# Stick-breaking attention with filler projections: the order of transpositions, first scores, filler and meta weights in a hybrid decoder layer

## The chip, the cores and the metric

The kernel runs on one core of a Trainium2 chip. The metric is device time in microseconds (us) of one execution. Engines are named as the profile names them: PE (TensorE, matrix products and transpositions), PEld (its weight loads), DVE (VectorE), ACT (ScalarE), POOL (GpSimd), SP (SyncE, which issues the DMA transfers).

## What is computed

One layer of a hybrid decoder: a sequence of 512 tokens with 16 learned meta tokens put in front (528 rows), width 1024, all in float32. The input is normalised and projected by `w_in`. From the projections, a gated chunkwise retention with 4 heads and a stick-breaking attention with 16 heads of width 64 are made; each passes an output projection and is multiplied by a sigmoid gate of its own, the sum goes through `w_out`, and a SwiGLU FFN follows. The change touches only the part in which the attention is computed, and the gate projections that are computed beside it:

```
def stick_breaking(q, k, v):
    ...
    for i in range(Lp // CHUNK):
        ...
        z = jnp.einsum('bhtd,bhsd->bhts', q_blk, k_pre) * scale
        ...
        log_not = jnp.where(valid, jax.nn.log_sigmoid(-z), 0.0)
        after = lax.cumsum(log_not, axis=3, reverse=True) - log_not
        a = jnp.where(valid, jnp.exp(jax.nn.log_sigmoid(z) + after), 0.0)
        outs.append(jnp.einsum('bhts,bhse->bhte', a, v_pre))
```

Each block of 128 queries attends to all keys before it, the 16 meta tokens among them. A weight is the sigmoid of its own score times the product of the sigmoids of the negated scores of all keys between it and the query.

## The kernel before

**Numbers in two halves.** TensorE multiplies in a short format here, so each float32 operand is split into a high half (ACT copies it, L104) and a low half (DVE subtracts, L101), and one product becomes three matmuls: high by high, low by high, high by low. One such group of three, for 128 of the depth, is called a triple here. A weight arrives by a DMA into `raw`, and its halves are `wh` and `wl`. In the scores, `ka` and `qa` are high halves of keys and queries and `kl` is the low half of the keys; only two matmuls are needed per score, since a tile of 128 rows holds both halves of a head of 64.

**A head.** The sixteen heads are taken as eight pairs; (p, h) below is half h of pair p. For a head there are four scores, one for each query block, from the longest (block 3, 528 keys, in two matmul pairs, since a bank holds 512 numbers) to the shortest (block 0, 144 keys). `score` (L600) does one: the matmuls on PE into banks `px`, sigmoids of the score and of its negative on ACT (L623, L624), a scan on DVE that makes the running products (L626), and a product on DVE that makes the weights `sp` (L627). `turn` (L644) transposes the weights on PE into a bank `pb` (L98), which ACT and DVE split into `ah` and `al`. `turn_meta` (L630) does the weights of the 16 meta keys apart: POOL copies and subtracts them into the tile `mg`, DVE transposes it into `x` (L639), POOL copies the result into `am`. `values` (L654) multiplies with the values on PE, and ACT and DVE add the two halves into `ysb` (L663, L664). Banks: `px` has three, of which the longest score takes two and each of the others and each value product one; `pb` has two.

**The order of the work.** PE would stand while DVE and ACT work on a score, so `head` (L692) writes out one head's transpositions and value product and the next head's scores as one list of pieces, each with a weight, and `run` (L807) places filler between the pieces in proportion to the weights: triples of projections, which need nothing of attention. z is a score, t a transposition, tm the meta weights, pv the value product; the number is the block:

```
            q, g = (p, 1) if hd == 0 else (p + 1, 0)
            seq = (
                (1.0, z, 3), (1.3, t, 3), (1.3, t, 2), (1.3, z, 2), (0.2, t, 1), (0.8, z, 1), (1.2, tm, 0), (1.8, t, 0),
                (1.4, z, 0), (1.2, pv, 0),
            )
```

So in the list of a first half (p, 0) the scores are those of (p, 1), and in that of a second half (p, 1) they are those of the next pair, (p + 1, 0). The filler comes from a queue of work (`Work`, L351), one item after the other. It holds, for each pair, the projections named in `FILL` (L778) for that pair, and then q and k of the pair after next (`qk_work`, L503). The items "b1", "b2" are gate projections of one block of 128 features (`gate_work`, L547: 8 triples, a sigmoid L555 and a store L556), "b45" and the like are gates of two blocks at once (`gates_work`, L560), and "v" is half of the values of two pairs. An item's weight is loaded when the item ahead of it begins. Before the loop over pairs (L817) an opening run (L816) computes the four scores of head (0, 0) with 8 triples of filler, of which 3/7 stand ahead of the first score. In pair 7 there is no next pair: both heads' pieces are one list, with what remains of the filler, and "a2" is left over for the time behind it. In pairs 1 to 5, `tm` also issues token sums on POOL, which a later stage needs.

From here to the end of attention PE's instructions stand in the order in which the code issues them. On DVE, ACT, POOL and SP a scheduler orders them. Behind attention, the sums `ysb` are split into `yh` and `yl`, and the projection by `w_sb_out` follows.

## Time and profile before

| what | value |
|---|---|
| median of 3 runs | 1211.29 us (1210.54 to 1212.5) |
| the profiled execution's own time | 1211.73 us |
| its span, from the first instruction to the last | 1209.9 us |
| mean granted clock of TensorE | 0.991 of full speed |
| scan L626, 64 of them | 59.8 us of DVE, 936 ns each on average |
| splits of weights `wl<-raw,wh` L101, 202 of them | 267.9 us of DVE, 1335 ns each on average |
| traffic of the DMA | 118.26 MB, mean 98 GB/s |

An engine's share says how much of the span it was busy; a DMA-issuing, waiting or branching instruction isn't counted as busy. In the lists of a timeline a line has the start of an instruction, its length, the engine, the line of code, the operation, what it writes and reads, and in brackets how long the engine had stood before it and which instruction ended that. The granted clock is the share of full speed at which TensorE was allowed to run: at half of it a matmul takes twice as long.

### The profile page before, as it was taken

The numbers are of one execution on the slowest core, as the hardware profiler recorded it, in microseconds if no ns is written. First come the engines' busy times: TensorE is split into PE (matmuls) and PEld (weight loads), VectorE is DVE, ScalarE is ACT, GpSimd is POOL, SyncE is SP. The second block draws the span as 40 slices with busy tenths as digits, with TensorE's granted clock in tenths as the row PEclk, the third lists the DMA queues.
The fourth block names the chain that finished last, engine by engine and source line by source line (L and its number), as shares of the span: only waits on it lengthen the run. The fifth ranks groups of instructions, "written<-read, shape, count | busy, mean of one in ns | idle before, by whom it ended". The sixth has DMA issues, their size and how long they took to land.

```text
span 1209.9 us, 18875 instructions
## 1 busy us (share of the span) xinstructions
PE 1174.2 (97%) x7629; PEld 1067.0 (88%) x7629; DVE 869.3 (72%) x1138; ACT 537.1 (44%) x905; POOL 387.2 (32%) x386
## 2 busy tenths in 40 slices
PE   7989999999999999999999999999999999999997
PEld 7877898889789998998899899778999999998886
DVE  6588898987536785586678657776899999983333
ACT  5477676755424434343333424334454444443221
POOL 2036668552032330340323020000265666620000
PEclk9989999999999999999999999999999999999999
DMA  6321211214643214132321425324222333353211
GB/s 194 86 72 53 70 48 41 70 45 139 213 138 130 70 46 138 36 95 89 105 71 45 139 70 154 133 87 157 71 80 95 106 105 106 108 178 114 94 46 70
DMA packets 94504, 118.26 MB, mean 98 GB/s; under 512 B 2488, under 2 KB 71104, under 8 KB 94416
## 3 DMA queue, kind: packets, MB, share of 16 engines
q1 hardware_dynamic: 93984, 115.98, 29.5%
q8 instruction: 60, 0.98, 0.3%
q10 hardware_dynamic: 432, 1.07, 0.3%
q14 instruction: 28, 0.23, 0.1%
HBM read 109.96 MB, written 7.08 MB: 97 GB/s over the span
## 4 chain that ended last, share of the span: by engine, by line
PE 77%; DVE 9%; POOL 3%; ACT 3%; issue 2%; DMA 1%; DVEq 0%; POOLq 0%; ACTq 0%; SPq 0%
PE pp L95 33%; PE pb L95 19%; PE pa L95 18%; PE pc L95 4%; DVE wl L101 3%; PE pb L98 2%; DVE sm L626 2%; PE px L95 2%; ACT wh L104 1%; DVE sp L627 1%; DMA raw<-in_w_in_dram 1%; POOL raw L260 1%; DVE kl L101 1%; POOL st L260 1%; DMA raw<-in_w_sb_out_dram 1%
## 5 line engine op out<-in xcount | busy, mean ns | idle before, releaser
L101 DVE TENSOR_TENSOR wl<-raw,wh 128x1024 fp32r<-128x1024 f32 (+1 forms) x202 | 267.9, 1335 | 78.7 <-ACT wh L104 75.2
L104 ACT ACTIVATE wh<-raw 128x1024 fp32r<-128x1024 f32 (+1 forms) x202 | 201.7, 1008 | 252.9 <-PE pp L95 85.7
L95 PE MATMUL pp<-hT,wh 128*128 128x512 f32 (+2 forms) x308 | 109.1, 354 | 1.4 <-DVE qb L101 1.2
L95 PE MATMUL pp<-hL,wh 128*128 128x512 f32 (+2 forms) x308 | 105.2, 342 | 0.0
L95 PE MATMUL pp<-hT,wl 128*128 128x512 f32 (+2 forms) x308 | 105.0, 341 | 0.0
L260 POOL TENSOR_TENSOR st<-raw 128x512 f32<-128x512 f32 x28 | 42.5, 1539 | 162.6 <-DMA raw<-in_w_in_dram 162.6
L101 DVE TENSOR_TENSOR wl<-st,wh 128x1024 fp32r<-128x1024 f32 x54 | 84.3, 1565 | 11.8 <-ACT wh L104 11.8
L95 PE MATMUL pp<-qk,wh 128*128 128x512 f32 x256 | 83.1, 399 | 2.0 <-ACT qk L104 1.7
L95 PE MATMUL pp<-wh,hT 128*128 128x256 f32 (+1 forms) x240 | 75.9, 317 | 0.7 <-ACT hT L104 0.7
L95 PE MATMUL pp<-wh,hL 128*128 128x256 f32 (+1 forms) x240 | 74.8, 312 | 0.8 <-DVE ss L147 0.8
L95 PE MATMUL pp<-wl,hT 128*128 128x256 f32 (+1 forms) x240 | 74.4, 310 | 0.0
L104 ACT ACTIVATE wh<-st 128x1024 fp32r<-128x1024 f32 x54 | 55.9, 1055 | 33.6 <-POOL st L260 20.5
L148 POOL TENSOR_TENSOR rs<-rs,nhalf 128x1 f32<-128x1 f32 x20 | 12.4, 618 | 171.0 <-DVE rs L147 171.0
L95 PEld LDWEIGHTS pp<-hT,wh 128*128 128x128 f32 x308 | 59.6, 193 | 7.0 <-issue 1.8
L626 DVE TENSOR_TENSOR_SCAN sm<-sm,mask 128x528 f32<-128x528 f32 (+1 forms) x64 | 59.8, 936 | 8.1 <-ACT sm L623 7.8
L95 PEld LDWEIGHTS pp<-hT,wl 128*128 128x128 f32 x308 | 59.4, 193 | 6.3
L95 PEld LDWEIGHTS pp<-hL,wh 128*128 128x128 f32 x308 | 59.5, 193 | 4.1
L95 PE MATMUL pa<-hL,wh 128*128 128x264 f32 (+1 forms) x192 | 61.6, 321 | 0.0
L95 PE MATMUL pa<-hT,wl 128*128 128x264 f32 (+1 forms) x192 | 61.6, 321 | 0.0
L95 PE MATMUL pa<-hT,wh 128*128 128x264 f32 (+1 forms) x192 | 61.6, 321 | 0.0
L95 PEld LDWEIGHTS pp<-qk,wh 128*128 128x128 f32 x256 | 47.6, 188 | 13.4 <-ACT qk L104 2.4
L101 DVE TENSOR_TENSOR gl<-gt,gh 128x512 fp32r<-128x512 f32 x22 | 16.0, 732 | 50.0 <-ACT gh L104 49.9
(333 smaller groups left out, 3845.8 us busy)
## 6 DMA issues: line engine op xcount, KB each, us to landing
raw<-in_w_in_dram SPq DMA_DIRECT2D x31, 1024.0 KB, 5.1
raw<-in_w_ffn_in_dram SPq DMA_DIRECT2D x22, 1024.0 KB, 5.1
raw<-in_w_in_dram SPq DMA_DIRECT2D x26, 512.0 KB, 4.1
raw<-in_w_ffn_out_dram SPq DMA_DIRECT2D x11, 1024.0 KB, 5.0
raw<-in_w_ret_out_dram SPq DMA_DIRECT2D x8, 1024.0 KB, 5.1
raw<-in_w_sb_out_dram SPq DMA_DIRECT2D x4, 1024.0 KB, 7.2
raw<-in_w_out_dram SPq DMA_DIRECT2D x4, 1024.0 KB, 5.1
ysb<-in_x_dram SPq DMA_DIRECT2D x4, 512.0 KB, 8.6
```

What stands on the lines that cost most here:

```text
L95: return keep(nc.tensor.matmul(*args, **kw))
L98: return keep(nc.tensor.transpose(dst, src, idn))
L101: nc.vector.tensor_tensor(lo, src, hi.bitcast(F32), op=ALU.subtract)
L104: ins = nc.scalar.activation(hi, src, AF.Copy)
L148: nc.gpsimd.tensor_tensor(dst, dst, nhalf[:n], op=ALU.pow)
L260: nc.gpsimd.tensor_tensor(d[:, k : k + 2], p[:, k : k + 2], q[:, k : k + 2], op=op)
L626: nc.vector.tensor_tensor_scan(rev, rev, mask[:, r0:][:, ::-1], 0.0, op0=ALU.mult, op1=ALU.max)
L627: nc.vector.tensor_tensor(sp, sp, sm[:, r0 + 1 : L + 1], op=ALU.mult)
```

## The change

It has three parts. **(1)** The opening run gets two projections' worth of filler instead of one: the gate "b0" goes ahead of q and k of pair 1, twice the columns are placed between the scores of (0, 0), and "b3" moves from the end of pair 7 to pair 0. **(2)** In the list of a second half, the transpositions t3 and t2 stand ahead of the next pair's first score z3 instead of behind it; the weight of each piece goes with it. **(3)** `turn_meta` becomes two functions: `split_meta`, the work of POOL into `mg`, is called behind the last score of a head, and `turn_meta` keeps the transposition on DVE and POOL's copies, at the place of `tm`.

```
-        def turn_meta(hd, att):
+        def split_meta(att):
             g = s2.tile([P, NT, 32], F32R, tag="mg", name="mg", bufs=1)
-            x = s2.tile([P, NT, 32], F32, tag="vs", name="x", bufs=1)
             for i in range(0, NT, 2):
...
                 nc.gpsimd.tensor_copy(g[:, two, 0:NM], m)
                 nc.gpsimd.tensor_tensor(g[:, two, NM:], m, g[:, two, 0:NM].bitcast(F32), op=ALU.subtract)
+            return g
+
+        def turn_meta(hd, g):
+            x = s2.tile([P, NT, 32], F32, tag="vs", name="x", bufs=1)
             nc.vector.transpose(x.rearrange("p a b -> p (a b)"), g.rearrange("p a b -> p (a b)").bitcast(F32))
...
         def z(p, hd, i):
             atts[p][hd][i] = score(p, hd, i)
+            if i == 0:
+                metas[p][hd] = split_meta(atts[p][hd])
...
         def tm(p, hd, j):
-            turn_meta(hd, atts[p][hd])
+            turn_meta(hd, metas[p][hd])
...
-            seq = (
-                (1.0, z, 3), (1.3, t, 3), (1.3, t, 2), (1.3, z, 2), (0.2, t, 1), (0.8, z, 1), (1.2, tm, 0), (1.8, t, 0),
-                (1.4, z, 0), (1.2, pv, 0),
-            )
+            ahead = ((1.0, z, 3), (1.3, t, 3), (1.3, t, 2)) if hd == 0 else ((1.3, t, 3), (1.3, t, 2), (1.0, z, 3))
+            seq = (*ahead, (1.3, z, 2), (0.2, t, 1), (0.8, z, 1), (1.2, tm, 0), (1.8, t, 0), (1.4, z, 0), (1.2, pv, 0))
...
-        FILL = [["b0"], ["b1"], ["v"], ["v"], ["v"], ["v"], ["b2"], ["b45", "b67", "a01", "b3"]]
+        FILL = [["b3"], ["b1"], ["v"], ["v"], ["v"], ["v"], ["b2"], ["b45", "b67", "a01"]]
...
         work = Work()
+        fill(work, 0, ["b0"])
         qk_work(work, 1)
...
-        run([(3.0, lambda: None)] + [(1.0, lambda i=i: z(0, 0, i)) for i in (3, 2, 1, 0)], KD * 3 * T)
+        run([(3.0, lambda: None)] + [(1.0, lambda i=i: z(0, 0, i)) for i in (3, 2, 1, 0)], 2 * KD * 3 * T)
```

What this does to the order of the instructions is shown at three places. A name's number tells one tile from another of the same name; the numbers differ between the two kernels.

The first place is DVE in the opening, from the second score's scan on. `sm` is a score's sigmoid, with the scan's result in it, and `sp` the weights; 528, 400, 272 and 144 columns are blocks 3, 2, 1 and 0. Before:

```order
L627 TENSOR_TENSOR sp_713<-sp_713,sm0_126 128x528
L626 SCALAR_TENSOR_TENSOR sm1_128<-sm1_128,mask_118 128x400
L626 SCALAR_TENSOR_TENSOR sm2_130<-sm2_130,mask_118 128x272
L627 TENSOR_TENSOR sp_713<-sp_713,sm1_128 128x400
L626 SCALAR_TENSOR_TENSOR sm0_126<-sm0_126,mask_118 128x144
L627 TENSOR_TENSOR sp_736<-sp_736,sm2_130 128x272
L627 TENSOR_TENSOR sp_736<-sp_736,sm0_126 128x144
L101 TENSOR_TENSOR wl_1121<-raw_1118,wh_1120 128x1024
L639 STREAM_TRANSPOSE x_859<-mg_858 128x128
```

And after the change:

```order
L627 TENSOR_TENSOR sp_722<-sp_722,sm0_126 128x528
L101 TENSOR_TENSOR wl_1095<-raw_1092,wh_1094 128x1024
L626 SCALAR_TENSOR_TENSOR sm1_128<-sm1_128,mask_118 128x400
L627 TENSOR_TENSOR sp_722<-sp_722,sm1_128 128x400
L626 SCALAR_TENSOR_TENSOR sm2_130<-sm2_130,mask_118 128x272
L627 TENSOR_TENSOR sp_764<-sp_764,sm2_130 128x272
L626 SCALAR_TENSOR_TENSOR sm0_126<-sm0_126,mask_118 128x144
L627 TENSOR_TENSOR sp_764<-sp_764,sm0_126 128x144
L643 STREAM_TRANSPOSE x_897<-mg_782 128x128
L101 TENSOR_TENSOR wl_1160<-raw_1157,wh_1159 128x1024
```

Each scan is now followed by its own product, and two splits of weights, in place of one, stand between the first product and the next thing that DVE does for head (0, 0): one of them behind the first product, the other behind the transposition of the meta weights.

The second place is PE at the start of the list of the second half (6, 1), behind the value product of (6, 0). `px<-ka,qa` and `px<-kl,qa` are the scores of (7, 0), `pb<-ident,sp` transpositions of (6, 1), `pp` filler. Before:

```order
L95 MATMUL px_3045<-ka_2927,qa_2915 128x264
L95 MATMUL px_3045<-kl0_134,qa_2915 128x264
L95 MATMUL px_3048<-ka_2927,qa_2915 128x264
L95 MATMUL px_3048<-kl0_134,qa_2915 128x264
L95 MATMUL pp_3026<-hT_83,wh_2923 128x512
L95 MATMUL pp_3026<-hL_84,wh_2923 128x512
L95 MATMUL pp_3026<-hT_83,wl_2924 128x512
L98 MATMUL pb_3061<-ident_73,sp_2842 128x128
L95 MATMUL pp_3026<-hT_83,wh_2923 128x512
L95 MATMUL pp_3026<-hL_84,wh_2923 128x512
L95 MATMUL pp_3026<-hT_83,wl_2924 128x512
L98 MATMUL pb_3070<-ident_73,sp_2842 128x128 x2
```

And after:

```order
L98 MATMUL pb_3084<-ident_73,sp_2881 128x128
L95 MATMUL pp_3065<-hT_83,wh_2962 128x512
L95 MATMUL pp_3065<-hL_84,wh_2962 128x512
L95 MATMUL pp_3065<-hT_83,wl_2963 128x512
L98 MATMUL pb_3093<-ident_73,sp_2881 128x128 x2
L95 MATMUL pp_3065<-hT_83,wh_2962 128x512
L95 MATMUL pp_3065<-hL_84,wh_2962 128x512
L95 MATMUL pp_3065<-hT_83,wl_2963 128x512
L95 MATMUL px_3103<-ka_2966,qa_2954 128x264
L95 MATMUL px_3103<-kl0_134,qa_2954 128x264
L95 MATMUL px_3106<-ka_2966,qa_2954 128x264
L95 MATMUL px_3106<-kl0_134,qa_2954 128x264
```

The two transpositions, with the triples that belong to them, now stand ahead of z3, whose four matmuls come last here. The next instruction after this piece is the second score of (7, 0), `px_3116<-ka_2966,qa_2954 128x400`, with no triple between; before, the triples and the transpositions lay between the two scores.

The third place is DVE at the end of pair 7. `go` is a gate projection's sum, `al` the low half of a transposition of (7, 1), and the two `wl` splits belong to `w_sb_out`, the weight of the stage behind attention. Before:

```order
L101 TENSOR_TENSOR wl_3649<-raw_3646,wh_3648 128x1024
L101 TENSOR_TENSOR al_3599<-pb_3594,ah_3598 128x384
L573 TENSOR_TENSOR go_3508<-pp_3590,go_3508 128x512
L101 TENSOR_TENSOR wl_3699<-raw_3696,wh_3698 128x1024
L101 TENSOR_TENSOR wl_3703<-raw_3696,wh_3702 128x1024
L101 TENSOR_TENSOR al_3640<-pb_3634,ah_3639 128x512
L664 TENSOR_TENSOR ysb_99<-px_3668,ysb_99 64x512
```

And after:

```order
L101 TENSOR_TENSOR al_3596<-pb_3591,ah_3595 128x384
L573 TENSOR_TENSOR go_3553<-pp_3615,go_3553 128x256
L101 TENSOR_TENSOR al_3631<-pb_3625,ah_3630 128x512
L573 TENSOR_TENSOR go_3553<-pp_3638,go_3553 128x2x256
L101 TENSOR_TENSOR wl_3699<-raw_3696,wh_3698 128x1024
L101 TENSOR_TENSOR wl_3703<-raw_3696,wh_3702 128x1024
L668 TENSOR_TENSOR ysb_99<-px_3662,ysb_99 64x512
```

The last `al`, with 512 columns, now stands ahead of the two splits, instead of behind them.

More of the change, by code (lines that the diff above doesn't have):

```diff
@@ L674, in hybrid_block @@
         turned_w = [({}, {}) for _ in range(NPAIR)]
+        metas = [{} for _ in range(NPAIR)]
         def z(p, hd, i):
             atts[p][hd][i] = score(p, hd, i)
+            if i == 0:
+                metas[p][hd] = split_meta(atts[p][hd])
         def t(p, hd, j):
```

## The prediction

> **What bounds the kernel now.** I read the page first, then the busy time by stretches, PE's order of time through attention (58 to 304 us), the waits, and at last DVE's order of time at the places where PE stands. The first part of the page:
>
> ```profile
> PE 1174.2 (97%) x7629; PEld 1067.0 (88%) x7629; DVE 869.3 (72%) x1138; ACT 537.1 (44%) x905; POOL 387.2 (32%) x386
> ```
>
> PE bounds the kernel: a microsecond in which PE stands is a microsecond of the time, if nothing later absorbs it. All three edits lie in attention. Below, a head is named (pair, half); each row runs from one head's value product to the next one's, for the seven second halves (0,1) to (6,1), then for (7,0) and (7,1). The columns are: length, then PE, PEld, DVE, ACT and POOL busy, granted clock, DMA.
>
> ```profile
> 80.33:89.69 9.36, 9.30 (x51) 7.54 (x50) 8.53 (x15) 7.57 (x23) 5.00 (x8) 1.00 0.35 114
> 106.02:115.71 9.69, 9.06 (x52) 7.62 (x50) 8.74 (x14) 6.44 (x16) 7.36 (x11) 1.00 0.18 54
> 135.05:144.68 9.63, 9.21 (x74) 8.84 (x73) 8.76 (x16) 7.63 (x19) 7.59 (x11) 1.00 0.33 109
> 162.00:173.28 11.28, 10.92 (x88) 10.56 (x87) 10.20 (x17) 8.28 (x23) 9.39 (x12) 1.00 0.01 1
> 189.45:202.10 12.65, 10.80 (x74) 10.43 (x72) 10.86 (x18) 9.04 (x24) 10.77 (x16) 0.87 0.14 42
> 218.13:230.96 12.83, 10.90 (x89) 10.54 (x88) 11.93 (x23) 8.79 (x25) 6.00 (x10) 1.00 0.40 133
> 247.45:260.22 12.77, 10.88 (x52) 8.88 (x51) 10.67 (x20) 8.84 (x25) 3.38 (x8) 0.87 0.26 82
> 260.22:284.11 23.89, 23.89 (x198) 23.76 (x197) 21.07 (x30) 12.51 (x25) 14.16 (x15) 1.00 0.16 57
> 284.11:300.58 16.47, 16.34 (x120) 15.36 (x119) 10.07 (x16) 8.16 (x12) 2.99 (x8) 1.00 0.53 168
> ```
>
> In the second halves both engines are nearly full: DVE is idle for 0.83, 0.95, 0.87, 1.08, 1.79, 0.90 and 2.10 us, 8.5 us together. So a head cannot get shorter there by more than that, however PE's work is placed. Where PE stands in attention, in order of time:
>
> ```profile
> 73.09 0.90 PE L98 MATMUL pb<-ident,sp 128*128 128x128 f32 x3 [3.42 <-DVE al L101]
> 109.36 0.39 PE L95 MATMUL px<-kl,qa 128*128 128x264 f32 x1 [0.63 <-DVE kl L101]
> 118.98 0.50 PE L95 MATMUL px<-al,vt 128*128 128x512 f32 x1 [1.27 <-DVE al L101]
> 138.59 0.39 PE L95 MATMUL px<-kl,qa 128*128 128x264 f32 x1 [0.42 <-DVE kl L101]
> 165.47 0.39 PE L95 MATMUL px<-kl,qa 128*128 128x264 f32 x1 [0.36 <-DVE kl L101]
> 194.46 0.39 PE L95 MATMUL px<-kl,qa 128*128 128x264 f32 x1 [1.85 <-DVE kl L101]
> 223.18 0.39 PE L95 MATMUL px<-kl,qa 128*128 128x264 f32 x1 [1.93 <-DVE kl L101]
> 252.31 0.39 PE L95 MATMUL px<-kl,qa 128*128 128x264 f32 x1 [1.86 <-DVE kl L101]
> 303.40 0.50 PE L95 MATMUL px<-al,vt 128*128 128x512 f32 x1 [1.07 <-DVE al L101]
> ```
>
> Six waits of 7.05 us in all are the first scores of the next pair waiting for kl, the low half of k. The longest wait is the first one, 3.42 us: the third transposition of head (0,0) needs the bank that al empties. Some waits cost more than their length, as the granted clock (the eighth number) shows in stretches of 4 us:
>
> ```profile
> 74.00:78.00 4.00, 4.00 (x20) 4.00 (x20) 3.31 (x7) 1.16 (x4) 0.46 (x2) 0.50 0.00 0
> 78.00:82.00 4.00, 4.00 (x24) 3.74 (x24) 2.30 (x4) 3.04 (x7) 0.00 (x0) 0.87 0.02 4
> 118.00:122.00 4.00, 3.02 (x11) 2.51 (x12) 3.43 (x7) 2.78 (x7) 1.69 (x4) 0.75 0.19 70
> 122.00:126.00 4.00, 4.00 (x17) 3.12 (x16) 2.92 (x5) 0.66 (x2) 3.80 (x6) 0.82 0.44 129
> 194.00:198.00 4.00, 3.54 (x18) 3.54 (x19) 3.94 (x6) 1.69 (x6) 3.71 (x7) 0.64 0.45 131
> 198.00:202.00 4.00, 4.00 (x34) 4.00 (x33) 3.77 (x7) 2.80 (x8) 3.92 (x5) 0.94 0.00 0
> 222.00:226.00 4.00, 2.83 (x23) 2.83 (x24) 3.55 (x7) 1.68 (x6) 3.24 (x7) 1.00 0.74 239
> ```
>
> The wait of 1.85 us is followed by 4 x 0.36 + 4 x 0.06 = 1.7 us of lost clock, the one of 1.27 us by 4 x 0.25 + 4 x 0.18 = 1.7 us. The longest wait of the six, 1.93 us, is followed by none. So a wait of 1.3 us or more may cost 1.7 us on top, and may not. Behind the 3.42 us the clock is at half from 73.09 to about 78.9 us, which costs (78.9 - 73.09) / 2 = 2.9 us.
>
> **The change part by part.** *Two projections beside the first scores.* The first pair's scores now have 16 triples (three matmuls of one step of a projection) beside them instead of 8. What one costs, and what paces DVE there:
>
> ```profile
> 57.67 0.39 PE L95 MATMUL pp<-hT,wh 128*128 128x512 f32 x1
> 60.46 0.28 PE L95 MATMUL px<-ka,qa 128*128 128x264 f32 x1
> 61.15 0.39 PE L95 MATMUL px<-kl,qa 128*128 128x264 f32 x1 [0.17 <-DVE kl L101]
> 80.33 0.39 PE L95 MATMUL px<-am,vm 128*128 128x512 f32 x1
> ```
>
> ```profile
> 62.94 1.26 DVE L626 TENSOR_TENSOR_SCAN sm<-sm,mask 128x528 f32<-128x528 f32 x1 [1.38 <-ACT sm L623]
> 67.84 1.21 DVE L101 TENSOR_TENSOR wl<-raw,wh 128x1024 fp32r<-128x1024 f32 x1
> 69.69 0.31 DVE L639 STREAM_TRANSPOSE x<-mg 128x128 f32<-128x128 f32 x1 [0.64 <-POOL mg L638]
> 72.75 0.62 DVE L101 TENSOR_TENSOR al<-pb,ah 128x128 fp32r<-128x128 f32 x2
> ```
>
> ```profile
> 60.65 1.28 ACT L623 ACT_TABLE_LOAD   x1
> ```
>
> Four triples take 60.46 - 57.67 = 2.79 us, so eight take 5.6. PE would have reached the third transposition at 73.09 - 3.42 = 69.7; now it is there at 69.7 + 5.6 - 0.4 = 74.9 (three more triples ahead of the first score also cover the kl wait at 61.15, about 0.4 us with what lies around it). DVE empties the first bank at about 73.05 before. Now its first scan starts some 1.0 us later (the score is 2.1 us later, but before ACT was loading its table until 61.93 and could not have read it sooner), and the order puts one more wl of 1.2 us in front: 75.3 at the earliest. The copies of q wait for the second projection as well, so I take 75.7 (up to 76.2). The wait shrinks from 3.42 to 0.8 us (0.4 to 1.3), below those that were followed by half clock. From there to the value product PE needs 80.33 - 73.09 - 2.9 = 4.3 us: 80.0 instead of 80.33, with 5.6 us more work done. Head (0,1) has 8.53 us of DVE work in 9.36 and gives nothing more, so the 0.3 us may be lost again. I take -5.5 (bounds -3 and -6.3, which is the whole of 3.42 + 2.9). What is moved is b3's projection, from the end of pair 7 to pair 0, and b0's ahead of q of pair 1. Their weights are there in time: they stand in the same places of SP's queue as those of q and k did. SP's store of b0 now stands ahead of a load, but its sigmoid is done long before.
>
> *What pair 7 gives back.* The moved 5.6 us counts only if pair 7 gets shorter by it. Of the weights in `head`, 11.5 of 18.5 lie in (7,0), so 3.45 us go there and 2.1 us in and behind (7,1). In (7,1) DVE has 16.47 - 10.07 us to spare. In (7,0) it has 23.89 - 21.07 = 2.8, and one sum of products and one half split now come after the last al. It fits, barely. I take +0.5 (0 to +3.45).
>
> *Transpositions ahead of the next pair's scores.* Three transpositions and two to three triples, about 1.3 to 1.6 us of work that needs no kl, now cover the wait. But what was cover later is gone: DVE between kl and the last al of that head has the same instructions as before, so PE meets al at the end of the head. For (6,1):
>
> ```profile
> 252.76 0.68 DVE L664 TENSOR_TENSOR ysb<-px,ysb 64x512 f32<-64x512 f32 x1
> 255.09 0.68 PE L95 MATMUL px<-ka,qa 128*128 128x400 f32 x1
> 259.91 0.68 DVE L101 TENSOR_TENSOR al<-pb,ah 128x512 fp32r<-128x512 f32 x1
> ```
>
> Here a new wait comes too: the second score follows the first with nothing between, and its bank is the one that the value product's sum ysb empties at 253.4; behind it stands the whole head. Of the 8.5 us that DVE is idle in the seven heads, the waits for mg stay:
>
> ```profile
> DVE x L639 <- POOL mg L638: 8.0, 13, 1.2
> ```
>
> At 0.43 to 0.64 us in most of the heads that is some 3.3 us in these seven. Of the remaining 5.2 us I take two thirds, -3.4 (0 to -5.2): most in (6,1), nothing in (2,1), where DVE is gapless between kl and al, and nothing in (5,1), where the order now puts a wl in front of kl.
>
> *New half-clock stretches.* Waits of 1 to 2.4 us now stand at the value products of (1,1), (2,1) and (4,1), in front of a first half, where PE had no wait at all. (1,1) had its stretch before. At 1.7 us and about even chances in the others I add +2.0 (0 to +5.1). The Trainium skill, "TensorE: Matmul & The Clock Gate", section "Why this matters for your kernels", says that only gaps of over about 3 us lose the clock; the rows at 118 and 194 disagree. By that page of the skill this term would be nothing, and the sum -9.4.
>
> *Meta weights split earlier.* In the order POOL's splits stand where they stood, behind the last score's product; the scheduler had already put them there, and POOL waits for that product, not for its own turn. DVE's transposition stands mostly right behind that product as before. I take 0 (0 to -1).
>
> *The end of pair 7.* In the 1.07 us at 303.40 al stood behind two splits that waited for a weight:
>
> ```profile
> 300.38 2.36 DVE L101 TENSOR_TENSOR wl<-raw,wh 128x1024 fp32r<-128x1024 f32 x2 [2.17 <-ACT wh L104]
> ```
>
> In the new order al comes first: -1.0 (0 to -1.07).
>
> Sum: -5.5 + 0.5 - 3.4 + 2.0 + 0 - 1.0 = -7.4 us. The profiled execution took 1211.73 (span 1209.9), 0.44 above the median of 1211.29. So 1211.29 - 7.4 = 1203.9.
>
> **The rivals.** *The wait moves and the clock goes with it (slower).* If the value products of six more second halves wait over 1.3 us, each following first half loses 1.7 us, +10.2, and the heads themselves gain nothing, since DVE sets their length. With -5.5, +0.5 and -1.0: +4.2, 1215.5. It decides from about five such heads on. For it: DVE's shares above. Against: in three of the heads the wait taken away is 0.36 to 0.63 us, too small to become 1.3. *Pair 7 does not get shorter.* If DVE bounds (7,0), 3.45 us stay instead of 0.5, and if the other heads gain nothing: -5.5 + 3.45 + 2.0 - 1.0 = -1.1, 1210.2. *The clock holds.* If no new wait costs clock, the term of 2.0 falls away: 1211.29 - 9.4 = 1201.9. The stretch behind 223.18 speaks for it, the three others against. By the rule of the Trainium skill named above it would come out so. *The waits are simply gone.* If DVE follows everywhere: 7.05 us and the two stretches of 1.7 in (4,1) and (6,1), whose clock is 0.87 above: -5.5 - 10.4 - 1.0 = -16.9, 1194.4; DVE's 8.5 us stand against it.
>
> **How the numbers follow.** The forecast has 0.52, the clock that holds 0.17, the waits gone 0.08, pair 7 not shorter 0.13, slower 0.10. The range leaves out the slower case and the one with all waits gone, 0.18 together: from the forecast with the better ends of the heads, the clock and the opening, 1203.9 - 1.8 - 2.0 - 0.8 = 1199.3, to pair 7's 1210.2, each with the 0.75 us by which the runs before lie apart: 1198.5 to 1211.0. About 0.2% (2.4 us) is what a measurement of this kernel can tell: faster 0.52 + 0.17 + 0.08 = 0.77, same 0.13, slower 0.10.
>
> **What would show it.** Right: the wait for al before (0,0)'s third transposition under 1.3 us and full clock from 70 to 80 us; kl waits under 0.8 us except in (5,1); instead of them waits of PE for al or ysb in the second halves; mg waits about 8 us as before; value products of pair 7 some 5 us closer together; nothing but a shift behind 304 us. Wrong: a stall of 2 us or more in the opening, half clock at the start of four first halves, or DVE idle time in the second halves that stays at 8 us.

## The result and the profile after

The changed kernel takes 1200.34 us (median of 4 executions, 1200.14 to 1202.83), the kernel before 1211.7 (4 executions, 1210.54 to 1212.5). The ratio is 0.9913, with a 95% interval of 0.9898 to 0.9927: 10.5 us less (8.8 to 12.4), worked out from the ratio; the medians lie 11.4 us apart. The forecast was 1203.9, with a range of 1198.5 to 1211.0. From one profiled execution to the other the span falls by 11.4 us, from 1209.9 to 1198.5. First the engines and the granted clock of the changed kernel:

```profile
PE 1166.4 (97%) x7629; PEld 1060.3 (88%) x7629; DVE 868.8 (72%) x1138; ACT 536.2 (45%) x905; POOL 384.7 (32%) x386
core 0: 1198.5 us, clock 0.999
```

The work is the same (7629 matmuls as before), and PE is busy for 7.8 us less. The granted clock goes with it: 0.991 of full speed before, 0.999 now. A matmul at half clock counts as busy, so lost clock looks like work. Next come the second halves (0,1) to (6,1) and the two heads of pair 7, in the same columns as in the prediction, each from the value product of the head ahead of it to its own:

```profile
81.02:89.83 8.81, 8.81 (x52) 7.55 (x51) 8.23 (x16) 7.21 (x23) 2.47 (x6) 1.00 0.36 119
106.41:115.59 9.18, 9.04 (x51) 7.61 (x50) 8.14 (x13) 5.91 (x16) 6.77 (x10) 1.00 0.20 57
133.69:142.79 9.10, 9.10 (x74) 8.84 (x73) 8.17 (x14) 7.24 (x19) 6.89 (x11) 1.00 0.36 117
160.92:171.57 10.65, 10.65 (x88) 10.50 (x87) 9.74 (x17) 8.18 (x23) 8.27 (x12) 1.00 0.01 2
189.12:199.64 10.52, 9.46 (x73) 8.89 (x72) 8.85 (x16) 8.83 (x24) 8.73 (x13) 1.00 0.18 52
217.24:227.89 10.65, 10.65 (x89) 10.49 (x87) 9.33 (x18) 8.18 (x23) 4.88 (x10) 1.00 0.31 101
244.39:255.01 10.62, 9.30 (x51) 7.67 (x50) 9.59 (x18) 8.72 (x25) 3.19 (x7) 1.00 0.30 99
255.01:275.71 20.70, 20.70 (x172) 20.56 (x170) 19.06 (x29) 12.63 (x25) 11.39 (x14) 1.00 0.11 31
275.71:290.96 15.25, 14.48 (x117) 13.95 (x116) 10.90 (x17) 6.30 (x10) 6.72 (x10) 1.00 0.46 145
```

The last three second halves are each 2.1 to 2.2 us shorter; (0,1) to (3,1) only 0.5 to 0.6. In (5,1), 12.83 us with 0.90 us of DVE idle before, the gain is over twice that idle time: the bound that the prediction put there is broken. DVE's own work between the two marks fell from 11.93 to 9.33 us, because part of it now lies on the other side of a mark (23 instructions between the marks before, 18 now). So it is in all seven: together they are 8.7 us shorter (78.2 to 69.5), but DVE's work in them fell by 7.6 (69.7 to 62.1), and its idle time only from 8.5 to 7.5. These rows alone don't show what the heads gain.

The waits of PE in attention, as sums (us in total, times, longest), show where they went:

```profile
PE px L95 <- DVE al L101: 5.5, 5, 1.5
PE pb L98 <- DVE al L101: 1.5, 2, 1.2
PE px L95 <- DVE ysb L668: 1.2, 2, 0.8
PE px L95 <- DVE kl L101: 1.1, 2, 0.6
```

The 7.05 us of waits for kl have become 1.1, and in their place stand 5.5 us for al and 1.2 for ysb. The longer ones one by one:

```profile
76.49 0.55 PE L98 MATMUL pb<-ident,sp 128*128 128x128 f32 x3 [1.20 <-DVE al L101]
119.16 0.50 PE L95 MATMUL px<-al,vt 128*128 128x512 f32 x1 [1.25 <-DVE al L101]
146.04 0.50 PE L95 MATMUL px<-al,vt 128*128 128x512 f32 x1 [1.54 <-DVE al L101]
174.12 0.50 PE L95 MATMUL px<-al,vt 128*128 128x512 f32 x1 [1.11 <-DVE al L101]
194.25 0.39 PE L95 MATMUL px<-kl,qa 128*128 128x264 f32 x1 [0.62 <-DVE kl L101]
202.35 0.51 PE L95 MATMUL px<-al,vt 128*128 128x512 f32 x1 [1.28 <-DVE al L101]
250.53 0.45 PE L95 MATMUL px<-ka,qa 128*128 128x400 f32 x1 [0.79 <-DVE ysb L668]
```

The opening's wait is 1.20 us instead of 3.42. At the value products of (1,1) to (4,1) PE waits 1.1 to 1.5 us. None of these waits is followed by half clock in this execution. So the waits for kl have mostly moved. All of PE's waits between 57 and 345 us together fell from 14.0 to 9.9 us, of which 2.2 is the opening's and 1.1 the one at the end of pair 7; the half clock behind them is gone altogether in this execution.

**A better ruler.** A head's end on PE can hide a wait, so the experiments below are read by the distance between the last al of two heads (128x512, the low half of the last transposition) on DVE. An example, (4,1) and (5,0), of before and then of the changed kernel:

```profile
202.31 0.66 DVE L101 TENSOR_TENSOR al<-pb,ah 128x512 fp32r<-128x512 f32 x1
218.06 0.67 DVE L101 TENSOR_TENSOR al<-pb,ah 128x512 fp32r<-128x512 f32 x1
```

```profile
201.62 0.68 DVE L101 TENSOR_TENSOR al<-pb,ah 128x512 fp32r<-128x512 f32 x1
215.41 0.67 DVE L101 TENSOR_TENSOR al<-pb,ah 128x512 fp32r<-128x512 f32 x1
```

218.06 - 202.31 = 15.75 us for (5,0) before, 215.41 - 201.62 = 13.79 now. All such distances, worked out in the same way from each kernel's profile (us; a star marks a head with a stretch of half clock in or just ahead of it; the names are those of the experiments):

| head | before | changed | p2 | d1 | t1 | h1 | h4 | h6 |
|---|---|---|---|---|---|---|---|---|
| (1,0) | 13.66 | 13.79 | 13.79 | 13.67 | 13.67 | 13.78 | 13.68 | 13.66 |
| (1,1) | 14.17 | 13.78 | 13.80 | 14.18 | 14.15 | 13.79 | 14.16 | 14.18 |
| (2,0) | 15.05* | 13.69 | 15.06* | 15.08* | 15.07* | 13.68 | 15.07* | 15.08* |
| (2,1) | 12.57 | 13.20 | 13.20 | 12.59 | 12.57 | 13.20 | 12.59 | 12.58 |
| (3,0) | 14.31 | 14.28 | 14.28 | 14.31 | 14.31 | 14.28 | 14.31 | 14.31 |
| (3,1) | 13.41 | 13.80 | 13.81 | 13.41 | 13.40 | 13.80 | 13.42 | 13.41 |
| (4,0) | 15.03 | 15.02 | 15.04 | 15.03 | 15.03 | 15.03 | 15.05 | 15.03 |
| (4,1) | 13.69* | 13.21 | 13.21 | 13.71 | 13.68* | 13.68* | 13.20 | 13.68* |
| (5,0) | 15.75 | 13.79 | 13.79 | 15.75 | 13.24 | 15.76 | 13.78 | 15.75 |
| (5,1) | 12.40 | 12.41 | 12.40 | 12.40 | 15.07 | 11.97 | 12.84 | 12.40 |
| (6,0) | 16.69 | 16.35 | 16.36 | 16.68 | 16.34 | 16.34 | 16.68 | 16.70 |
| (6,1) | 12.76* | 10.99 | 11.00 | 11.75 | 13.04* | 11.73 | 11.74 | 10.98 |

Where nothing near was changed, the numbers of this table repeat to 0.03 us from kernel to kernel. The heads' gain, -5.18 us in the second column, is no even one: -1.36 in (2,0), -1.96 in (5,0), -1.77 in (6,1), -0.48 in (4,1), -0.39 in (1,1), -0.34 in (6,0), and +0.63 and +0.39 in (2,1) and (3,1).

### The profile page after: what moved, and what is told of

It is laid out like the page before. It is cut to its first block, busy times and chain, and to the rows that moved or that the text cites. A ratio compares the mean times of both kernels' runs of the same rounds, so it can differ in the third digit from the quotient of the medians.

```text
span 1198.5 us, 18879 instructions
## 1 busy us (share of the span) xinstructions
PE 1166.4 (97%) x7629; PEld 1060.3 (88%) x7629; DVE 868.8 (72%) x1138; ACT 536.2 (45%) x905; POOL 384.7 (32%) x386
## 4 chain that ended last, share of the span: by engine, by line
PE 76%; DVE 10%; issue 4%; POOL 3%; ACT 2%; DMA 0%; DVEq 0%; POOLq 0%; ACTq 0%; SPq 0%
PE pp L95 33%; PE pa L95 17%; PE pb L95 17%; PE pc L95 5%; DVE wl L101 3%; DVE sm L626 2%; PE pb L98 2%; PE px L95 2%; DVE sp L627 1%; DVE al L101 1%; ACT wh L104 1%; POOL raw L260 1%; POOL st L260 1%; DVE kl L101 0%; POOL am L646 0%
## 5 line engine op out<-in xcount | busy, mean ns | idle before, releaser
L101 DVE TENSOR_TENSOR wl<-raw,wh 128x1024 fp32r<-128x1024 f32 x202 | 268.3, 1336 | 74.9 <-ACT wh L104 71.6
L104 ACT ACTIVATE wh<-raw 128x1024 fp32r<-128x1024 f32 x202 | 201.7, 1008 | 251.4 <-PE pp L95 87.1
L101 DVE TENSOR_TENSOR wl<-st,wh 128x1024 fp32r<-128x1024 f32 x54 | 85.4, 1585 | 11.5 <-ACT wh L104 11.4
L148 POOL TENSOR_TENSOR rs<-rs,nhalf 128x1 f32<-128x1 f32 x20 | 12.4, 619 | 171.0 <-DVE rs L147 171.0
```

The lines of the kernel that those rows point to most:

```text
L101: nc.vector.tensor_tensor(lo, src, hi.bitcast(F32), op=ALU.subtract)
L104: ins = nc.scalar.activation(hi, src, AF.Copy)
L148: nc.gpsimd.tensor_tensor(dst, dst, nhalf[:n], op=ALU.pow)
```

## The experiments

In each, time is compared with the kernel before on the same chip; the ratio has its 95% interval behind it. Its medians there were 1210.94 us (17 executions, p1 to d1), 1210.83 (35, t1 to s0), 1210.19 (16, h4 to v1) and 1211.15 (9, v2). A difference in us is worked out from the ratio; the difference of the medians can be up to 1.5 us another. In the edits, `(...)` stands for the orders shown in p2: the first one is that of the kernel before, the second has the transpositions ahead.

**p1: part (1) alone.** The kernel before with

```
-        FILL = [["b0"], ["b1"], ["v"], ["v"], ["v"], ["v"], ["b2"], ["b45", "b67", "a01", "b3"]]
+        FILL = [["b3"], ["b1"], ["v"], ["v"], ["v"], ["v"], ["b2"], ["b45", "b67", "a01"]]
...
+        fill(work, 0, ["b0"])
         qk_work(work, 1)
...
-        run([(3.0, lambda: None)] + [(1.0, lambda i=i: z(0, 0, i)) for i in (3, 2, 1, 0)], KD * 3 * T)
+        run([(3.0, lambda: None)] + [(1.0, lambda i=i: z(0, 0, i)) for i in (3, 2, 1, 0)], 2 * KD * 3 * T)
```

> Part (1) alone: twice the filler beside the first scores, b0 ahead, b3 moved to pair 0; parts (2) and (3) undone. By the prediction's terms it gives -5.5 for the opening, +0.5 given back in pair 7 and -1.0 at its end: -6.0 us, 0.995 of the time before. The clock theory (most of the gain of the change is half-clock time that is gone, not waiting time) expects about the same, split otherwise: 2.2 us of the wait of 3.42 us and 3.4 us of half clock in the opening, 1.1 at the end of pair 7, -6.7 us; the waits for kl in the second halves stay at 1.8 to 1.9 us from (4,1) on, and some of them are followed by a stretch of half clock of 3.4 us. If parts (1) and (2) depend on each other, this run and the next don't add up to the -11.4 us of the whole.

Measured: 1203.8 us, 0.9948 (0.9932 to 0.9964), -6.3 us. The opening's wait is 1.22 us, as in the whole change, and the opening has no half clock. The prediction's three terms for this part hold as a sum, -6.0; the clock theory's -6.7 lies within the interval too. The waits for kl stayed, two of them with half clock behind, as the clock theory expected.

**p2: part (2) alone.** The kernel before with

```
-            seq = (
-                (1.0, z, 3), (1.3, t, 3), (1.3, t, 2), (1.3, z, 2), (0.2, t, 1), (0.8, z, 1), (1.2, tm, 0), (1.8, t, 0),
...
+            ahead = ((1.0, z, 3), (1.3, t, 3), (1.3, t, 2)) if hd == 0 else ((1.3, t, 3), (1.3, t, 2), (1.0, z, 3))
+            seq = (*ahead, (1.3, z, 2), (0.2, t, 1), (0.8, z, 1), (1.2, tm, 0), (1.8, t, 0), (1.4, z, 0), (1.2, pv, 0))
```

> Part (2) alone: the two transpositions ahead of the next pair's first score in the second halves; opening as before, so its wait of 3.42 us and its half clock stay. By the prediction's terms -3.4 for the heads and +2.0 for new half clock: -1.4 us. By the clock theory the waits only move (kl falls from 7.05 to about 1 us, al and ysb rise by about 5 us), but the half clock behind them goes: three stretches of 1.7 us in the profiled execution of before, 2.3 in the mean over executions if a stretch depends on where a wait falls: -4 to -5 us, 0.996 to 0.997, with no granted clock under 1.00 between 90 and 300 us except perhaps behind the value products of (1,0) and (2,0).

Measured: 1205.68 us, 0.996 (0.9946 to 0.9975), -4.8 us where the prediction's terms make -1.4. This is where the forecast was short. The clock theory's -4 to -5 has the number, but t1 and h4 below show that 2 us of it have another cause. The heads behave as in the whole change, but for a stretch of half clock in (2,0), so parts (1) and (2) add up: -6.3 - 4.8 = -11.1. This profile holds a surprise too, in the opening, which part (2) leaves alone: PE waits there even longer, 3.72 us, and no half clock follows at all. We come back to it.

**p12: parts (1) and (2) without part (3).** The kernel before with the edits of p1 and p2 together; that is, in the changed kernel:

```
         def z(p, hd, i):
             atts[p][hd][i] = score(p, hd, i)
-            if i == 0:
-                metas[p][hd] = split_meta(atts[p][hd])
...
-            turn_meta(hd, metas[p][hd])
+            turn_meta(hd, atts[p][hd])
```

> Parts (1) and (2) without part (3): the meta weights are copied and split in the place of before in the code. The prediction gave part (3) 0 (0 to -1 us). Expected: the time of the changed kernel, 1200.3 us within its own scatter, 0.991 of the time before. A part (3) that matters would leave it over 2.4 us slower than the changed kernel, with longer waits of DVE's transposition x for POOL's mg.

Measured: 1199.93 us, 0.9918 (0.9903 to 0.9933), as the changed kernel. There was nothing to find: on every engine its profile has the changed kernel's instructions in the same order, so the scheduler puts POOL's splits in the same place wherever the code calls them. Part (3) changes no order at all here. One thing is to be kept in mind: in this profile (2,0) took 15.07 us, with half clock, where that of the changed kernel has 13.69 without. The same order keeps this stretch or loses it from execution to execution.

**d1: useless work in the waits for kl.** The kernel before with (p is here the pair whose scores are computed, so the places are (4,1), (5,1) and (6,1))

```
             for cs in parts:
                 z = bank_x()[:, :w]
+                for _ in range(12 if p >= 5 and hd == 0 and i == 3 and cs.start == 0 else 0):
+                    mm(z, q[:, ts_], kk[:, cs], start=True, stop=True)
                 mm(z, q[:, ts_], kk[:, cs], start=True, stop=False)
```

> The kernel before, with useless work in three waits: the first product of z3 (128x264, ka by qa) is computed 12 times more, 12 x 0.117 = 1.4 us, in front of the product that waits for kl, in the second halves (4,1), (5,1) and (6,1), where PE waits 1.85, 1.93 and 1.86 us. The clock theory: the wait shrinks to some 0.45 us, nothing starts earlier, but no half clock follows: -3.4 us against the profiled execution of before, in which two of the three waits were followed by it, -3.2 in the mean if each is followed by it in about 0.6 of the executions. The rival, that the clock isn't what is paid there or that it is lost by something other than PE's standing: 0 to +0.5 us. If the repeats delay the scores (kl not last), slower by up to 4 us.

Measured: 1209.44 us, 0.9999 (0.9986 to 1.0012). The first half of the clock theory came true, the second did not. PE in the places concerned:

```profile
195.09 0.39 PE L95 MATMUL px<-kl,qa 128*128 128x264 f32 x1 [0.47 <-DVE kl L101]
203.68 0.50 PE L95 MATMUL px<-al,vt 128*128 128x512 f32 x1 [1.10 <-DVE al L101]
223.82 0.39 PE L95 MATMUL px<-kl,qa 128*128 128x264 f32 x1 [0.72 <-DVE kl L101]
252.98 0.39 PE L95 MATMUL px<-kl,qa 128*128 128x264 f32 x1 [0.73 <-DVE kl L101]
303.45 0.49 PE L95 MATMUL px<-ah,vt 128*128 128x512 f32 x1 [2.02 <-ACT ah L104]
```

The waits shrank as worked out and no half clock follows them. But in (4,1) the clock that was saved came back as a wait of 1.10 us for al, where before had none: the distance from al to al is 13.71, against 13.69 with half clock. There half clock cost nothing, since DVE set the pace. In (6,1) it did cost, 12.76 - 11.75 = 1.0 us. What that should have brought was lost at the end of pair 7 in this execution (1213.88 us, one of the slowest of twelve, 1207.15 to 1213.92), where ah stood behind splits of `w_sb_out` (the 2.02 us) that had waited 5.68 us for their weight, against 3.02 in before.

**t1: ACT's split th out of the way.** Where, then, did (5,0) lose its 1.96 us? Not on PE: ACT's time at q's weight in (5,0), first before and then in the changed kernel (th is the split of the token sums, which waits for POOL):

```profile
211.84 1.06 ACT L184 ACTIVATE th<-go 128x1024 fp32r<-128x1024 f32 x1 [1.37 <-POOL go L175]
212.81 1.05 ACT L104 ACTIVATE wh<-raw 128x1024 fp32r<-128x1024 f32 x1
```

```profile
209.78 1.06 ACT L104 ACTIVATE wh<-raw 128x1024 fp32r<-128x1024 f32 x1 [0.20 <-PE pp L95]
212.33 1.05 ACT L184 ACTIVATE th<-go 128x1024 fp32r<-128x1024 f32 x1
```

Before, th stood ahead of wh and held it up for its own wait and its own length; now it stands behind, and by then POOL is done. The edit to the kernel before moves POOL's sums of (5,0), and th with them, to (5,1):

```
-                for _ in range(6):
+                for _ in range({(5, 0): 0, (5, 1): 12}.get((p, hd), 6)):
                     next(token_sums, None)
```

> The kernel before, with one thing moved: the six token sums that tm issues on POOL in head (5,0) are issued in (5,1). With that, ACT's split th (L184), which waits 1.37 us for POOL, no longer stands ahead of the split wh of q's weight in (5,0); PE's and SP's orders stay, DVE's differs by one exchange. Theory of the order: a good part of what the heads gain by the change is this split, which the scheduler puts behind wh in the changed kernel. Then the low half al of (5,0)'s last transposition comes 13.8 us behind that of (4,1) instead of 15.75, and the kernel is 2.0 us faster (0.9984). Rival: th's place has no price, since the wait of DVE for wh is hidden under PE's work; 0 us. If th then holds up ah in (5,1), up to +1.4 us.

Measured: 1211.11 us, 1.0001 (0.9988 to 1.0015): no gain. But (5,0) fell from 15.75 to 13.24 us, 2.5 us, and (5,1) rose from 12.40 to 15.07, where th now waits ahead of ah:

```profile
225.94 1.06 ACT L184 ACTIVATE th<-go 128x1024 fp32r<-128x1024 f32 x1 [1.54 <-POOL go L175]
226.91 0.47 ACT L104 ACTIVATE ah<-pb 128x384 fp32r<-128x384 f32 x1
```

So a th that stands ahead costs some 2 us or more, and the experiment only carried the cost to the next head. That its place alone does it in (5,0), h4 has to show.

**h1: part (2) in five second halves.** p2 with

```
-            ahead = (...) if hd == 0 else (...)
+            ahead = (...) if hd == 0 or p in (4, 6) else (...)
```

> The kernel before, with part (2) in five of the seven second halves: (0,1), (1,1), (2,1), (3,1) and (5,1), not in (4,1) and (6,1). th stays ahead of wh in (5,0). By the prediction's account, that a wait for kl which goes is worth what DVE is idle there: up to -2 us, (5,1) nothing. By the theory of the order (part (2) alone moves waits, and its gain lies in th's place, which the exchange in (4,1) brings about, and in (6,1)): 0 us, +0.5 to -0.5, with waits for al of 1.1 to 1.5 us at the value products of (1,1), (2,1) and (3,1) in place of the waits for kl.

Measured: 1208.23 us, 0.9983 (0.9973 to 0.9994), -2.0 us: by time, what the prediction's account allows at most. The distances side with the order: apart from (2,0) and (6,1), which had no half clock here by chance (in (6,1) the wait for kl was still 1.86 us), they change by -0.05 us in sum over (1,0) to (6,1). The median gains nonetheless. I read it as clock, since the mean granted clock of its 12 executions is 0.9952, against 0.9926 of the 35 of before beside it; it is argued from that, not shown. The argument is weak: the executions of d1 have the same mean clock, 0.9952, and gained nothing. What the -2.0 us are stays open.

**h4: part (2) in (4,1) alone.** p2 with

```
-            ahead = (...) if hd == 0 else (...)
+            ahead = (...) if (p, hd) != (4, 1) else (...)
```

> The kernel before, with part (2) in one second half alone, (4,1). In this order ACT's split th stands behind wh in (5,0), as in the changed kernel. Theory of the order: al of (5,0) comes 13.8 us behind that of (4,1) instead of 15.75, and (4,1) itself gains 0.5 us; the other heads keep their times: -2.4 us, 0.998. Rival, that each wait for kl that is covered is worth its length: -1.85 and its half clock of 1.7 us, up to -3.5, all of it between the value products of (4,0) and (4,1) and none in (5,0). Third: nothing, 0, as the repeats in front of kl gave nothing there.

Measured: 1206.2 us, 0.9968 (0.9956 to 0.998), -3.9 us. The distances say -2.4 as expected: (4,1) 13.20, (5,0) 13.78. So the exchange in (4,1) is what puts th behind wh, one head later, and the rival, which had all of the gain in (4,1) and none in (5,0), is out. All fourteen profiles go by th's place: (5,0) takes 15.74 to 15.76 us in the six with th straight ahead of wh (before, p1, d1, h1, d2, h6), 13.77 to 13.80 in the six with th behind (changed, p2, p12, h4, v1, v2), 15.18 in s0 with one ah between the two, and 13.24 in t1 without th. By time the gain is 1.5 us more than -2.4, which lies at the very edge of the interval. And (5,1) gave 0.44 us back (12.84). In this profile (6,1) had no half clock, 1.0 us by chance; the rest stays open.

**h6: part (2) in (6,1) alone.** p2 with

```
-            ahead = (...) if hd == 0 else (...)
+            ahead = (...) if (p, hd) != (6, 1) else (...)
```

> The kernel before, with part (2) in one second half alone, (6,1). The run with repeats in front of kl showed al of (6,1) 11.75 us behind that of (6,0) without half clock, against 12.76 with it; in the changed kernel it is 10.99. So -0.75 us for the transpositions and -1.0 for the half clock in executions that had it (about 0.6 of them): -1.4 us in the mean, 0.9989 (-0.7 to -1.8). th stays ahead of wh, so (5,0) keeps its 15.75.

Measured: 1208.46 us, 0.9986 (0.9975 to 0.9996), -1.7 us, and (6,1) at 10.98: as expected. This is the head in which the exchange itself saves most: 0.75 us, beside 1.0 of clock. (4,1) with 0.48 and (1,1) with 0.39 follow.

**d2: useless work in the opening's wait.** The kernel before with a piece of weight 0 ahead of the third transposition of (0,0):

```
+        def busy(p, hd, ns):
+            for n in ns:
+                z = bank_x()
+                for _ in range(n):
+                    mm(z, hT[:, 0, 0:P], hT[:, 0, NM : NM + T], start=True, stop=True)
...
+            if p == 0 and hd == 0:
+                seq = (*seq[:4], (0.0, busy, (6, 6, 2)), *seq[4:])
```

> The kernel before, with useless work in the opening's wait: 14 products of 128x512 (14 x 0.235 = 3.3 us, operand hT, results unused) ahead of the third transposition of head (0,0), where PE waits 3.42 us for al. The wait shrinks to about 0.2 us and no score, transposition or value product can start earlier through it except by the clock. If half clock there is paid in full, since PE and not DVE sets the end of that head (al is done 1.7 us ahead of the value product): -2.5 to -3 us against an execution with both stretches of half clock. If it is hidden, as in the second halves (where the repeats in front of kl gave nothing): 0. If the useless products wait for their banks and push the transposition back: up to +1 us.

Measured: 1208.68 us, 0.9986 (0.9975 to 0.9997), -1.7 us, less than the -2.5 to -3 expected. The opening kept its full clock. From its first triple (57.67 us in before, 56.86 here) to the value product of (0,0) (80.33, 77.33) it takes 20.47 us instead of 22.66: 2.2 us of the 2.9 that the prediction gave for the half clock. The time shows a little less. One reason may be in the profiles: of the seven with the old opening (before, p2, d1, t1, h1, h4, h6) four lost two windows of 3.41 us there, two lost one, and p2 none. Later in its own profile d2 lost time for other reasons: a scan in (3,0) took 1.61 us instead of 0.99 (the head 14.94), and (5,1) had half clock (13.81).

**s0: the balance of the two halves.** The changed kernel with

```
-        QK, SLACK = KD * 3 * (T + L), 2 * 3 * T
+        QK, SLACK = KD * 3 * (T + L), 0 * 3 * T
```

> The changed kernel with SLACK 0 instead of 2 triples: of each pair from 0 to 6 two triples (1.4 us) of filler move from the first half to the second. In the changed kernel al is done 0.7 to 1.8 us ahead of PE at the end of the first halves (1,0) to (5,0), and PE waits 1.1 to 1.5 us for al at the end of the second halves (1,1) to (4,1). If that unevenness is what is left of the waits: -2 to -4 us against the changed kernel (1196 to 1198). If k, whose projection then ends later, brings the waits for kl back, or DVE is full over a whole pair: 0 to +2 us against it. In this order th stands ahead of wh again (behind one ah), which by the theory of the order costs some 1 to 2 us of it.

Measured: 1207.62 us, 0.9979 (0.9968 to 0.9989): 7 us slower than the changed kernel by the medians, over three times the worst that I expected. From the last al of (0,1) to that of (6,1) it takes 170.8 us, where the changed kernel takes 164.3. The waits for kl are back, in spite of the transpositions ahead of them, and th stands ahead of wh again:

```profile
198.39 0.39 PE L95 MATMUL px<-kl,qa 128*128 128x264 f32 x1 [2.30 <-DVE kl L101]
226.47 0.39 PE L95 MATMUL px<-kl,qa 128*128 128x264 f32 x1 [0.93 <-DVE kl L101]
256.52 0.39 PE L95 MATMUL px<-kl,qa 128*128 128x264 f32 x1 [1.90 <-DVE kl L101]
```

**v1: part (2) only where it helps.** The changed kernel with

```
-            ahead = (...) if hd == 0 else (...)
+            ahead = (...) if hd == 0 or p in (2, 3) else (...)
```

> The changed kernel with part (2) undone in (2,1) and (3,1), where by the distances from al to al it made the heads longer (13.20 instead of 12.57, and 13.80 instead of 13.41). Theory: -1.0 us against the changed kernel (1199.4), with waits for kl of about 0.4 us there and for al of under 0.5 at their ends. Rival: the distances in (3,0) and (4,0) give it back: 0. This is less than the runs can tell from no change unless the profile shows it.

Measured: 1199.43 us, 0.9912 (0.9898 to 0.9925), not to be told from the changed kernel by time. In the profile (2,1), (3,0) and (3,1) take 12.59 + 14.31 + 13.42 = 40.32 us instead of 41.28, the 1.0 expected; (2,0) had its half clock, 15.07, which took it back.

**v2: and the clock kept at (1,1).** v1 with

```
+            for _ in range(5 if (p, hd) == (1, 1) else 0):
+                mm(y, vm[:, hl, :], both, start=True, stop=True)
             mm(y, vm[:, hl, :], both, start=True, stop=False)
```

> The changed kernel with part (2) undone in (2,1) and (3,1), as in the run before, and with useless work in one wait: the first product of (1,1)'s value product (128x512, am by vm) is computed 5 times more, 5 x 0.235 = 1.2 us, ahead of the product that waits 1.26 us for al. In that place a stretch of half clock followed in most profiles, and al of (2,0) then comes 15.07 us behind that of (1,1) instead of 13.69. Clock theory: the wait shrinks to about 0.1 us, the windows of 3.41 us around it are filled, no half clock between 60 and 300 us in any execution, (2,0) at 13.7: up to 1.4 us faster than the run without repeats where that had the stretch, 0.7 in the mean: 1198.7. Rival: the repeats delay the value product or the clock is lost all the same: 0 to +1.2 us.

Measured: 1197.83 us (1197.38 to 1199.21), 0.9902 (0.9884 to 0.992), the fastest median here, though its interval overlaps those of v1 and the changed kernel. Stretches of 4 us at that place, first v1 and then v2:

```profile
118.00:122.00 4.00, 3.79 (x13) 3.17 (x13) 3.40 (x7) 2.02 (x6) 2.36 (x5) 0.57 0.31 102
```

```profile
118.00:122.00 4.00, 4.00 (x21) 3.32 (x22) 3.40 (x6) 2.12 (x7) 2.72 (x5) 1.00 0.41 131
```

(2,0) takes 13.69 us instead of 15.07. All five executions have a mean clock of 0.999, those of v1 0.997 to 0.998. The wait itself hardly shrank (1.00 us for 1.26), since the repeats also filled smaller waits ahead of it, 0.15 us for al and 0.19 for ah. Useless work paid here, and not in (4,1), because in (2,0) PE sets the pace: its last al begins 1.7 us ahead of the value product in v1 (132.54 and 134.24), while in (4,1) of before it begins 0.2 us behind (202.31 and 202.10).

## Why the prediction was right, and where not

The difference of the two profiled spans, -11.4 us, falls into four pieces: +0.5 us ahead of the opening's first triple, -0.1 in the opening, -5.2 in the heads (1,0) to (6,1) and -6.65 behind them. Part (1) moved 5.6 us of work from the last piece to the second, so each of these two is read with that work set off.

- *The opening, -5.5.* From the first triple (57.67 before, 58.20 now) to the last al of (0,1) (90.42, 90.85) it takes 32.75 us before and 32.65 now, with 5.6 us more work: -5.7. The wait was put at 0.8 us (0.4 to 1.3) and is 1.20; DVE was to empty the bank at 75.7 (up to 76.2) and PE goes on at 76.49, of which 0.5 us is the later start of the whole stretch. The loss of 2.9 us of clock is gone. Right, with p1 and d2 behind it.
- *Pair 7 and its end, +0.5 and -1.0.* From the last al of (6,1) (259.91, 255.16) to the end of the span (1209.9, 1198.5) it is 949.99 us before and 943.34 now: -6.65, of which 5.6 is the work moved away. So -1.1 instead of -0.5.
- *Meta split, 0.* Right, and for a stronger reason than I gave: the order is the same on every engine.
- *The heads, -3.4, and new half clock, +2.0.* Together -1.4; measured -5.18 by the distances. Here the sum failed, in two steps. The step of new half clock failed in sign: the new waits at the value products stand there, 1.11 to 1.54 us, but none was followed by half clock in this execution, while stretches of before went away: -1.36 in (2,0), by chance (p12 had it), and -1.0 in (6,1). The step of the heads failed in its mechanism: without clock the heads gain 5.18 - 1.36 - 1.0 = 2.8 us, near the 3.4, but that is luck. Of it 1.96 is the place of th on ACT, an engine whose order I did not look at there. The exchange by itself, with all its gains and losses (-0.75 in (6,1), -0.48 in (4,1), -0.39 in (1,1), -0.34 in (6,0), +1.0 in (2,1) and (3,1)), leaves about -0.9: a wait that is covered was mostly paid again at the value product.
- *"So a head cannot get shorter there by more than that, however PE's work is placed."* This failed as well, in (4,1), (5,1) and (6,1). It holds for a stretch whose work on DVE is fixed; between two value products it isn't.
- *What would show it.* Waits for kl under 0.8 us, waits for al and ysb in their place and full clock in the opening came out; the value products of pair 7 moved together by 4.4 us, near the 5. But one sign of being wrong nearly came true too: DVE's idle time in the second halves was to fall well below 8 us, and it is 7.5 (8.5 before). (5,1), where I kept the wait for kl, lost it. The waits for mg were to stay at 8 us and are 5.8:

```profile
DVE x L643 <- POOL mg L637: 5.8, 10, 0.6
```

- *The rivals.* "The clock holds" was the nearest, 1201.9. The slower one had its waits only in part (1.1 to 1.5 us at four value products, one of them over its 1.3), and not its price. *"The waits are simply gone"* asked for -16.9 and is out.

## What to carry to other kernels

Lost clock hides in busy time: read the granted clock stretch by stretch, and price it only where PE sets the pace; where another engine did, in (4,1), half clock was free and the clock regained turned into a wait. A wait that is covered moves to the next thing that the same engine produces, so measure from one product of that engine to the next (al to al), not from mark to mark on the engine that waits. An edit of one engine's order lets a scheduler reorder the others: compare the order on every engine, one head further than the edit, before pricing the edit.

## What the runs showed of the hardware

When a wait costs clock can be told. The ends of the half-clock stretches of one execution lie multiples of 3.413 us apart (before: 79.03, 123.40, 198.50 and 256.52, with 13, 22 and 17 steps between). So time is cut into windows of 3.413 us, and the windows decide. In rows of such windows (the eighth number is the granted clock), of before:

```profile
68.79:72.20 3.41, 0.88 (x7) 0.67 (x6) 2.70 (x5) 2.69 (x9) 1.92 (x7) 1.00 0.52 149
72.20:75.62 3.42, 2.52 (x12) 2.53 (x13) 3.39 (x7) 1.14 (x3) 0.14 (x1) 0.50 0.02 5
75.62:79.03 3.41, 3.41 (x17) 3.41 (x17) 2.11 (x5) 0.60 (x1) 0.32 (x2) 0.50 0.00 0
218.97:222.39 3.42, 2.27 (x17) 1.98 (x15) 2.82 (x7) 3.03 (x8) 1.39 (x2) 1.00 0.27 91
222.39:225.80 3.41, 2.62 (x22) 2.63 (x23) 3.32 (x7) 1.61 (x5) 2.79 (x5) 1.00 0.80 259
```

and of p2, where the wait of 3.72 us lay:

```profile
67.69:71.10 3.41, 1.55 (x12) 1.34 (x11) 2.44 (x4) 3.38 (x11) 2.71 (x8) 1.00 0.31 86
71.10:74.51 3.41, 1.55 (x13) 1.55 (x14) 3.35 (x6) 0.98 (x4) 0.10 (x1) 1.00 0.23 68
```

In p2 the wait fell on two windows, 1.86 us in each, and neither cost anything; in before 2.53 us of the 3.42 fell in one window, and the next was at half clock. The wait of 1.93 us in (5,1) was split too, 1.15 and 0.78.

Idle time alone doesn't separate them: a window with 1.48 us of it was followed by half clock, one with 1.86 wasn't. What does is the number of columns that PE fed in a window, counted from PE's order of time (a matmul's columns, spread over the time to the next one's start). In the twelve profiles that have a stretch to fix the windows (all but those of the changed kernel and v2), 977 whole windows between 57 and 338 us give this:

| columns fed in a window | windows | next window at half clock |
|---|---|---|
| 792 to 2871 | 31 | 31 |
| 2948 to 7552 | 946 | 0 |

So here a window below some 38 to 39% of the most that one fed, 7552 columns, puts the next one at half clock (how a matmul beside a wait is spread shifts the two edges by up to some 50 columns). A window that is itself at half clock counts by what it fed: a gapless one feeds some 3600 or more and ends the stretch, one with a gap of 0.9 us (2634 in before, 72.20) prolongs it. The Trainium skill, "TensorE: Matmul & The Clock Gate", section "What's actually happening", has windows of 3413 ns that run freely; the trace agrees. Its section "Why this matters for your kernels" has the clock fall after idle gaps of over some 3 us; the runs here say otherwise, since a gap of 1.3 us in the wrong place is enough, and one of 3.7 us can go free.

The windows don't move with the kernel's waits, so the same wait costs 1.7 us of clock in one execution and none in another. How much of the changed kernel's clean execution is luck can be estimated: lay the windows over its PE order in steps of 5 ns and count where one falls below the bound. Behind (1,1) that is so at about 40% of the places, behind (2,1) at 19 to 27% (bound 2871 or 2948), behind (3,1) and (4,1) at none. In v2's order no place between 57 and 310 us has such a window.

I take the windows for part of the reason why executions of before differ by 8 us (1206.0 to 1214.0 in 35), with mean clocks of 0.990 to 0.996, and those of v2 by 1.8 (only five, all at 0.999). They aren't all of it: over the 35, time and mean clock correlate at -0.65.
